# The expert layer's first matrix in 512-column passes, with the product banks handed out in pairs

## The chip, the core and the metric

The kernel runs on one core of one Trainium2 chip. The metric is the device time of one execution in microseconds (us), the median of several runs. The engines are called PE (matrix product), PEld (its weight loads), DVE (vector), ACT (scalar), POOL and SP; a line number such as L95 is a line of the kernel before.

## What is computed

Two transformer blocks on 256 tokens of width 1024, in float32. The last layer of the second block is a layer of 16384 experts, of which each token takes 16 for each of 8 heads:

```python
def peer_ffn(x, w_query, sub_keys, expert_u, expert_v):
    def block(xb):
        q = (xb @ w_query).reshape(PEER_TOKEN_BLOCK, PEER_HEADS, 2, PEER_HALF)
        sc = jnp.einsum('thpd,hpkd->thpk', q, sub_keys)
        s_top, i_top = lax.top_k(sc, PEER_TOPK)
        ...
        u = jnp.take(expert_u, eidx, axis=0)
        h = jax.nn.gelu(jnp.einsum('thkd,td->thk', u, xb))
        vv = jnp.take(expert_v, eidx, axis=0)
        return jnp.einsum('thk,thkd->td', g * h, vv)
```

The kernel does not gather experts. It multiplies the input with the whole of `expert_u` (the expert layer's first matrix, `peer_u`), applies gelu, multiplies each value with the gate of its token and expert (zero for those not chosen), and multiplies the result with the whole of `expert_v` (the second layer).

## The kernel before

**Products.** Every float32 operand is split into a high and a low part of type fp32r. A product is three matmuls into one accumulation (`mm3`, L108 to L112): high weight by high input (L110), high weight by low input (L111), low weight by high input (L112). The weights come in units of 128x1024 values: a DMA on SP's queue brings `raw`, ACT copies it to `whi` (L95), DVE forms the difference `wlo` (L96). There are 4 buffers for `raw`. Of `whi` and `wlo` there are 3 buffers in each of two pools up to the end of the second block's mixing part, and 3 in one pool in the expert layer: there the `whi` of a unit takes the buffer of the unit three places before it. `gemm_t` (L117) runs one unit: 8 slices k of 128 rows, 24 matmuls of 256 columns (the 256 tokens). `gemm_n` (L141) has the parts the other way round: the input is the stationary operand, and 512 columns of weights stream through.

**Banks.** A product goes to a bank of 512 float32 columns. `mm_bank` (L99) hands out four banks in turn, each a tile of its own; `ax_bank` four more for transposes, scores and sums. A bank is read out ("evicted") by DVE or ACT.

**Order.** A compiler pass (a list scheduler) writes the final order of each engine's instructions from the order in the program, the buffers and its own idea of durations; a tile's new user waits for the tile's earlier readers. On the chip each engine takes its instructions in that written order and holds at one whose semaphore count is not reached.

**The expert layer.** `first_layer(j)` (L994) runs unit j of `peer_u` (128 units of 128 experts) by `gemm_t`, two units into the two 256-column halves of one bank; after the odd one ACT applies gelu and writes `S` (L1009). Between the units run 16 query products (`query`, L955; read out by ACT as `qT`, L969), the score products on them, and the steps by which DVE chooses the experts (`pump`, `all_steps`). When the choice is done (`ready`), one-hot products (L942) form the gates of the first 128 tokens four at a time (`form`, `combine`): DVE and ACT build the operands, and DVE and ACT write the results into `S`. In this part the gelu of a pair is in two pieces (L1006, L1009), and DVE multiplies (L1007). The second layer (L1069) is 1536 matmuls of 512 columns into four `ax` banks.

**Other places named below.** L330 reads out a unit of the gate product of the first block (`gate`), L397 the gate and up products of its feed-forward part (`gu`), L291 the query, key and value products, L363 and its like the outputs of a projection (`xT`).

Of the kernel before, what the change touches and what calls it, by code (L numbers as in the profile page):

```python
# [7 lines left out]
F32 = mybir.dt.float32  # L8
F32R = mybir.dt.float32r
# [3 lines left out]
AF = mybir.ActivationFunctionType  # L13
OP = mybir.AluOpType
# [14 lines left out]
T = 256  # L29
TH = 128  # L30
# [10 lines left out]
NSMALL = _o  # L41


class Net:
    def __init__(self, tc, a, out, stack):
        self.tc, self.nc, self.a, self.out, self.stack = tc, tc.nc, a, out, stack
        nc = self.nc
        self.const = self.pool("const", 1)
        self.psum = self.pool("psum", 1, space=PSUM)
        self.tiny = self.pool("tiny", 2)  # L50
        self.small = self.const.tile([128, NSMALL], F32, name="small")
        nc.scalar.dma_start(out=self.small, in_=a["small"])
        self.ones = self.const.tile([128, 128], F32, name="ones")
        nc.vector.memset(self.ones, 1.0)
        warm = self.const.tile([128, 1], F32, name="warm")
        nc.scalar.activation(warm, self.ones[:, 0:1], AF.Exp)
        ps = self.ax_bank()
        for _ in range(WARM):
            nc.tensor.matmul(ps[:, :128], lhsT=self.ones, rhs=self.ones, start=True, stop=True)
# [21 lines left out]
    def unit_(self, src, n, pieces, engine, between):  # L81
# [17 lines left out]
                self.last_low = low.ins  # L99
        return hi, lo  # L100

    def mm_bank(self):
        return self.psum.tile([128, 512], F32, name="mm", bufs=4)

    def ax_bank(self, dt=F32):
        return self.psum.tile([128, 512], dt, name="ax", bufs=4)
# [1 line left out]
    def mm3(self, ps, left, right, first, last):  # L108
        mm = self.nc.tensor.matmul
        mm(ps, lhsT=left[0], rhs=right[0], start=first, stop=False)  # L110
        mm(ps, lhsT=left[0], rhs=right[1], start=False, stop=False)  # L111
        mm(ps, lhsT=left[1], rhs=right[0], start=False, stop=last)  # L112

    def acts(self, hl, k, ts=slice(0, T)):
        return hl[0][:, k, ts], hl[1][:, k, ts]
# [91 lines left out]
        return r  # L207

    def new_acts(self, pool, K=8, tag="act", bufs=2):
        return (pool.tile([128, K, T], F32R, tag=tag + "h", name=tag + "h", bufs=bufs),  # L210
                pool.tile([128, K, T], F32R, tag=tag + "l", name=tag + "l", bufs=bufs))

    def load_const(self, pool, name, shape):
        t = pool.tile(shape, F32, name=name)
# [20 lines left out]
    def block1(self, actp):  # L235
        nc, a, tc = self.nc, self.a, self.tc
        mult, add, sub = OP.mult, OP.add, OP.subtract
        with ExitStack():
# [6 lines left out]
            first = self.unit_(a["w_in_a"][0], 1024, 4, nc.gpsimd, load_x)  # L245
            h = self.new_acts(actp)
# [8 lines left out]
            both = self.const.tile([128, 192], F16, name="iota16")  # L255
# [4 lines left out]
            with ExitStack() as s1:  # L260
                p = self.pool("mix", 1, s1)
# [10 lines left out]
                for i, (dst, sc) in enumerate(dests):  # L272
                    ps = (self.ax_bank() if i in (3, 4) else self.mm_bank())[:, :T]
                    parts = first if i == 0 else None
                    if i == 1 or i == 2:
                        parts = self.unit(a["w_in_a"][i], 1024, pieces=2)
# [7 lines left out]
                    if i == 2:  # L284
                        r = self.norm_column(acc, "ra")
                    if i < 4:
                        continue
                    if i == 4:
                        R = self.rows(r, "ra")
# [6 lines left out]
                    if i == 5:  # L296
                        ps = self.ax_bank()
# [3 lines left out]
                        nc.scalar.activation(av.rearrange("p a b -> p (a b)"), ps[:, :T], AF.Copy)  # L301

                both = self.xbp.tile([128, 8, T], F32R, tag="xbh", name="att", bufs=1)
                att = both[:, 0:4], both[:, 4:8]
                probs = [self.att1_probs(p, tb, aq, ak, mask) for tb in range(2)]
                rv = p.tile([128, 2, D], F32, name="rv")
                room = p.tile([128, 8, 512], F32, tag="gate", name="room")
# [19 lines left out]
                for i in range(16):  # L327
                    ps = self.mm_bank()[:, :T]
# [8 lines left out]
                for m in range(8):  # L337
                    if m % 2 == 0:
                        hi, lo = self.unit(a["w_att_o"][m // 2], 1024)
                    ps = self.mm_bank()  # L340
                    for k in range(4):
                        s = slice((m % 2 * 4 + k) * 128, (m % 2 * 4 + k) * 128 + 128)
# [9 lines left out]
                h = self.new_acts(actp)  # L352
                acc = self.work.tile([128, T], F32, name="acc")
                for m in range(8):
# [3 lines left out]
                    if m < 2:  # L358
                        ps = two[m]
                    else:  # L360
                        ps = self.mm_bank()[:, :T]
# [4 lines left out]
            with ExitStack() as s1:  # L366
                p = self.pool("ffn", 1, s1)
# [8 lines left out]
                for f in range(KF):  # L376
                    ps = self.mm_bank()
                    if f == 0:
                        other = self.mm_bank()
                        self.gemm_t_late([(ps[:, :T], a["w_gate"][0]), (other[:, :T], a["w_up"][0])], h)  # L380
                        r = self.norm_column(acc, "rb")
# [3 lines left out]
                    if f == 2:  # L385
                        R = self.rows(r, "rb")
# [7 lines left out]
                    for f0, (g, u) in enumerate(early, f + 1 - len(early)):  # L394
                        gu = p2.tile([128, 2, T], F32, name="gu")
                        if f0:
                            nc.vector.tensor_tensor(out=gu, in0=g, in1=R[:, None, :].to_broadcast([128, 2, T]),  # L397
                                                    op=mult)
# [10 lines left out]
                h = self.new_acts(actp)  # L409
                acc = self.work.tile([128, T], F32, name="acc")  # L410
                acg = self.work.tile([128, T], F32, name="acg")
                for m in range(8):
                    ps = self.mm_bank()[:, :T]
# [303 lines left out]
    def peer(self, st, x3, h, acc):  # L717
        nc, a, tc = self.nc, self.a, self.tc
        mult, add, sub = OP.mult, OP.add, OP.subtract
        with tc.using_default_side("right"):  # L720
# [3 lines left out]
            late = ExitStack()  # L724
            p = self.pool("topk", 1, late)
            pick = p.tile([128, 3, 128], F32, name="pick")
        xb = self.new_acts(self.xbp, tag="xb", bufs=1)
        hand = self.pool("hand", 2, st)
        x3t = tc.dram_tile([2, 128, D], F32, name="x3t")
        stop = p.tile([128, 4, 2, 2, 16], F32, name="stop")  # L730
# [134 lines left out]
        ready = False  # L865

        def pump(budget):
            nonlocal credit
            credit = min(credit, 0) + budget
            while credit > 0:  # L870
                step = next(steps, 0)
                if step == 0:
                    return True
                if step is None:
                    return False
                step[1]()
                credit -= step[0]
            return False

        bank = None  # L880
# [67 lines left out]
                nc.scalar.activation(S[:, jd:, t0:t0 + 4], C[:, jd:], AF.Copy, scale=1.0 / GSCALE)  # L948
            done += 4

        pair, keys, r, R = None, None, None, None
        waiting = []
        firsts = []

# [37 lines left out]
                    nc.scalar.dma_start(out=x3t[c, :, k4 * 512:k4 * 512 + 512], in_=xt)  # L992

        def first_layer(j):  # L994
            nonlocal pair
            e = j % 2
            if e == 0:
                pair = self.mm_bank()
            self.gemm_t(pair[:, e * T:e * T + T], a["peer_u"][j], xb, 8)
            if e == 0:  # L1000
                return
            js = slice(j - 1, j + 1)
            p3 = pair.rearrange("p (e t) -> p e t", e=2)
            if done:
                gt = gtp.tile([128, 2, TH], F32, name="gt")
                nc.scalar.activation(gt[:, :, :done], p3[:, :, :done], AF.Gelu_apprx_tanh)  # L1006
                nc.vector.tensor_tensor(out=S[:, js, :done], in0=S[:, js, :done], in1=gt[:, :, :done], op=mult)  # L1007
            if done < T:
                nc.scalar.activation(S[:, js, done:], p3[:, :, done:], AF.Gelu_apprx_tanh)  # L1009

        for c in range(RAWQ):
            query(c)
            ready = pump(PQ)
# [18 lines left out]
        for j in range(128):  # L1032
            first_layer(j)
            if c < 16 and j % QE == QE - 1:
                query(c)
                c += 1
                pump(PQ)
            elif c == 16 and waiting:
                for one in waiting:
                    score(*one)  # L1040
                waiting.clear()
            if not ready:
                ready = pump(PU)
                if ready:
                    start = j
                    with tc.using_default_side("right"):
                        gtp = self.pool("gelu", 2, groups)
                        cp = self.pool("comb", 1, hots)
                    ga = cp.tile([128, TH], F32, name="ga")
                    nc.scalar.activation(ga, gs[:, 0], AF.Copy)  # L1050
            elif j % 2 and not fill:
                while done < TH and (done + len(formed) * 4) * (GP - start) < TH * (j - start):
                    combine(j + 1)
                if done == TH:
                    hots.close()
                    with tc.using_default_side("right"):
                        gp = self.pool("gates", 1, groups)
                    fill = [fetch(4 * i) for i in range(3)]
            if j == 121:
                apply(0, fill.pop(0))  # L1060
# [12 lines left out]
        for j in range(128):  # L1073
            w = self.unit(a["peer_v"][j], 1024)
            s = [qp.tile([128, T], F32R, tag=t, name=t, bufs=n) for t, n in (("keys", 2), ("q", 3))]
# [109 lines left out]
```

## Time and profile before

| | us |
|---|---|
| median of 3 runs (lowest, highest) | 1287.78 (1287.43, 1288.07) |
| the profiled execution's own time | 1289.19 |
| its span, first to last instruction | 1287.4 |
| PE busy | 1276.2 |
| DVE busy | 904.6 |
| ACT busy | 718.7 |
| choice of experts running beside the first matrix | about 523 to 731 of the span |
| first matrix after the choice | about 731 to 935 |
| second layer | about 935 to 1283 |

A row of the timeline gives the start in us from the span's start, the duration, the engine, the line, the operation with the tile written and those read, the sizes, and in brackets how long the engine had been idle and what ended that. The end of a matmul is modelled and matmuls overlap, so what a matmul costs is read from the distance between two starts. A row of the stretches gives for each engine its busy time and instructions, then the granted clock of PE (1.00 is 2.4 GHz), the busy share of the DMA engines and GB/s.

### The profile page before, as it was taken

The numbers are of one execution on the slowest core, as the hardware profiler recorded it, in microseconds if no ns is written. First come the engines' busy times: TensorE is split into PE (matmuls) and PEld (weight loads), VectorE is DVE, ScalarE is ACT, GpSimd is POOL, SyncE is SP. The second block draws the span as 40 slices with busy tenths as digits, with TensorE's granted clock in tenths as the row PEclk, the third lists the DMA queues.
The fourth block names the chain that finished last, engine by engine and source line by source line (L and its number), as shares of the span: only waits on it lengthen the run. The fifth ranks groups of instructions, "written<-read, shape, count | busy, mean of one in ns | idle before, by whom it ended". The sixth has DMA issues, their size and how long they took to land.

```text
span 1287.4 us, 23568 instructions
## 1 busy us (share of the span) xinstructions
PE 1276.2 (99%) x9125; PEld 1186.8 (92%) x9125; DVE 904.6 (70%) x1785; ACT 718.7 (56%) x1158; POOL 269.4 (21%) x173
## 2 busy tenths in 40 slices
PE   8999999999999999999999999999999999999998
PEld 7878999999999889999999999999988888888887
DVE  7767677766666886988895566776566666666665
ACT  5455545545455675655554676666555555555553
POOL 2000000000000000008778887773000000000000
PEclk9999999999999999999999999999999999999999
DMA  7745668965567544567777777776677777777764
GB/s 261 230 131 153 179 188 293 335 195 184 177 186 221 160 145 138 182 187 186 181 168 209 181 169 177 165 172 173 215 217 221 217 215 218 219 219 220 215 199 160
DMA packets 90928, 253.02 MB, mean 197 GB/s; under 512 B 26944, under 2 KB 28736, under 8 KB 90688
## 3 DMA queue, kind: packets, MB, share of 16 engines
q1 hardware_dynamic: 68816, 241.45, 61.0%
q0 software_dynamic: 20992, 8.46, 5.9%
q8 instruction: 71, 1.16, 0.4%
q10 hardware_dynamic: 1008, 1.61, 0.3%
q14 instruction: 41, 0.34, 0.1%
HBM read 240.93 MB, written 10.55 MB: 195 GB/s over the span
## 4 chain that ended last, share of the span: by engine, by line
PE 93%; DVE 5%; issue 1%; DMA 0%; ACT 0%; SPq 0%; ACTq 0%; DVEq 0%
PE ax L1069 27%; PE mm L110 21%; PE mm L112 20%; PE mm L111 20%; DVE wlo L96 2%; PE ax L942 1%; DVE itop L741 1%; PE ax L888 0%; DMA xT<-in_xT_dram 0%; DVE stop L739 0%; ACT whi L95 0%; DVE sc L744 0%; DVE pos L741 0%; PE ax L678 0%; PE ax L713 0%
## 5 line engine op out<-in xcount | busy, mean ns | idle before, releaser
L96 DVE TENSOR_TENSOR wlo<-raw,whi 128x1024 fp32r<-128x1024 f32 (+2 forms) x433 | 524.4, 1213 | 239.6 <-ACT whi L95 238.2
L95 ACT ACTIVATE whi<-raw 128x1024 fp32r<-128x1024 f32 (+3 forms) x439 | 457.9, 1045 | 313.2 <-PE mm L111 219.6
L110 PE MATMUL mm<-xbh,whi 128*128 128x256 f32 x1104 | 312.0, 283 | 0.0
L112 PE MATMUL mm<-xbh,wlo 128*128 128x256 f32 x1104 | 308.3, 279 | 0.3 <-DVE wlo L96 0.2
L111 PE MATMUL mm<-xbl,whi 128*128 128x256 f32 x1104 | 308.3, 279 | 0.2 <-DVE xbl L155 0.2
L832 POOL DMA_INDIRECT cmat<-best,pos x128 | 241.6, 1887 | 226.4 <-DVE itop L741 164.6
L110 PE MATMUL mm<-acth,whi 128*128 128x256 f32 x848 | 239.4, 282 | 3.0 <-DVE qkv L291 1.4
L111 PE MATMUL mm<-actl,whi 128*128 128x256 f32 x848 | 237.9, 281 | 1.5 <-DVE actl L253 1.5
L112 PE MATMUL mm<-acth,wlo 128*128 128x256 f32 x848 | 237.0, 280 | 0.0
L112 PEld LDWEIGHTS mm<-xbh,wlo 128*128 128x128 f32 x1104 | 207.4, 188 | 1.3 <-DVE wlo L96 0.9
L111 PEld LDWEIGHTS mm<-xbl,whi 128*128 128x128 f32 x1104 | 207.6, 188 | 0.4 <-DVE xbl L155 0.4
L110 PEld LDWEIGHTS mm<-xbh,whi 128*128 128x128 f32 x1104 | 207.6, 188 | 0.2 <-ACT xbh L154 0.2
L110 PEld LDWEIGHTS mm<-acth,whi 128*128 128x128 f32 x848 | 159.9, 189 | 4.3 <-DVE qkv L291 1.7
L111 PEld LDWEIGHTS mm<-actl,whi 128*128 128x128 f32 x848 | 160.1, 189 | 2.2 <-DVE actl L253 2.2
L112 PEld LDWEIGHTS mm<-acth,wlo 128*128 128x128 f32 x848 | 160.0, 189 | 0.2 <-DVE wlo L96 0.2
L1069 PE MATMUL ax<-whi,q 128*128 128x512 f32 x512 | 158.0, 389 | 0.0
L1069 PE MATMUL ax<-whi,keys 128*128 128x512 f32 x512 | 157.9, 389 | 0.0
L1069 PE MATMUL ax<-wlo,keys 128*128 128x512 f32 x512 | 157.9, 389 | 0.0
L154 ACT ACTIVATE keys<-S 128x256 fp32r<-128x256 f32 x128 | 53.5, 418 | 151.4 <-PE ax L1069 151.4
L1069 PEld LDWEIGHTS ax<-whi,q 128*128 128x128 f32 x512 | 96.1, 188 | 20.0
L1069 PEld LDWEIGHTS ax<-wlo,keys 128*128 128x128 f32 x512 | 96.1, 188 | 19.9
L1069 PEld LDWEIGHTS ax<-whi,keys 128*128 128x128 f32 x512 | 96.0, 188 | 20.0
(282 smaller groups left out, 1405.5 us busy)
## 6 DMA issues: line engine op xcount, KB each, us to landing
raw<-in_peer_u_dram SPq DMA_DIRECT2D x128, 512.0 KB
raw<-in_peer_v_dram SPq DMA_DIRECT2D x128, 512.0 KB
raw<-in_w_in_b_dram SPq DMA_DIRECT2D x32, 512.0 KB
raw<-in_w_in_a_dram SPq DMA_DIRECT2D x31, 512.0 KB
raw<-in_w_gate_dram SPq DMA_DIRECT2D x22, 512.0 KB
raw<-in_w_up_dram SPq DMA_DIRECT2D x22, 512.0 KB
raw<-in_w_out_dram SPq DMA_DIRECT2D x16, 512.0 KB
cmat<-zero SPq DMA_DIRECT2D x16, 512.0 KB
```

What stands on the lines that cost most here:

```text
L95: self.last_copy = nc.scalar.activation(hi[:, s], raw[:, s], AF.Copy).ins
L96: low = (engine or nc.vector).tensor_tensor(out=lo[:, s], in0=raw[:, s], in1=hi[:, s].bitcast(F32), op=OP.subtract)
L110: mm(ps, lhsT=left[0], rhs=right[0], start=first, stop=False)
L111: mm(ps, lhsT=left[0], rhs=right[1], start=False, stop=False)
L112: mm(ps, lhsT=left[1], rhs=right[0], start=False, stop=last)
L154: nc.scalar.activation(hi, src, AF.Copy)
L741: yield cost + 50, lambda: nc.vector.max_index(where[:, o:o + 8], top[:, o:o + 8], vals)
L832: i = nc.gpsimd.indirect_dma_start(self.cmat, bass.IndirectOffsetOnAxis(ap=ps[:, hd, 1, k:k + 1], axis=0), bs[:, hd, 1, k:k + 1], None, co ...
L942: nc.tensor.matmul(C[:, t * 128:t * 128 + 128], lhsT=A[:, t], rhs=G[i][:, t], start=i == 0, stop=i == 1)
L1069: nc.tensor.matmul(banks[tb][d], lhsT=s[left][:, ts], rhs=w[right][:, d * 512:d * 512 + 512], start=first, stop=end)
```

## The change

Three things change.

First, the high and the low part of an input stand side by side in one tile, for each k 256 columns of the high part and then 256 of the low (`new_acts`, `xb`, `att`).

Second, from the end of the choice of experts on, `first_layer` runs a unit by `gemm_w`: for each k one matmul of 512 columns (high weight, both parts) and one of 256 (low weight, high part). The two halves of the bank are added at the end: ACT copies the right halves of a pair of banks to `gt`, and DVE adds the left halves (`added`). Gelu then reads `gt`.

Third, the four product banks become two tiles of two banks each (`mm_pair`), each tile used in turn; `mm_bank` hands out the first bank of such a tile, then the second. This holds for the whole kernel.

```diff
+        self.half = None
...
+    def mm_pair(self):
+        self.half = None
+        return self.psum.tile([128, 2, 512], F32, name="mm", bufs=2)
+
     def mm_bank(self):
-        return self.psum.tile([128, 512], F32, name="mm", bufs=4)
+        if self.half is None:
+            pair = self.mm_pair()
+            self.half = pair[:, 1]
+            return pair[:, 0]
+        bank, self.half = self.half, None
+        return bank
...
+    def mm2(self, ps, weight, acts, k, first, last):
+
+        mm = self.nc.tensor.matmul
+        both = acts[2][:, k]
+        mm(ps, lhsT=weight[0], rhs=both, start=first, stop=False)
+        mm(ps[:, :T], lhsT=weight[1], rhs=both[:, 0], start=False, stop=last)
+
+    def gemm_w(self, ps, src, hl, K, k0=0, first=True, last=True):
+
+        hi, lo = self.unit(src, K * 128)
+        for k in range(K):
+            s = slice(k * 128, k * 128 + 128)
+            self.mm2(ps, (hi[:, s], lo[:, s]), hl, k0 + k, first and k == 0, last and k == K - 1)
+
+    def added(self, out, pair):
+
+        self.nc.scalar.activation(out, pair[:, :, T:], AF.Copy)
+        self.nc.vector.tensor_tensor(out=out, in0=pair[:, :, :T], in1=out, op=OP.add)
...
     def new_acts(self, pool, K=8, tag="act", bufs=2):
-        return (pool.tile([128, K, T], F32R, tag=tag + "h", name=tag + "h", bufs=bufs),
-                pool.tile([128, K, T], F32R, tag=tag + "l", name=tag + "l", bufs=bufs))
+        both = pool.tile([128, K, 2, T], F32R, tag=tag, name=tag, bufs=bufs)
+        return both[:, :, 0], both[:, :, 1], both
...
-            nonlocal pair
+            nonlocal pair, wide
             e = j % 2
             if e == 0:
-                pair = self.mm_bank()
-            self.gemm_t(pair[:, e * T:e * T + T], a["peer_u"][j], xb, 8)
+                wide = ready
+                pair = self.mm_pair() if wide else self.mm_bank()
+            if wide:
+                self.gemm_w(pair[:, e], a["peer_u"][j], xb, 8)
+            else:
+                self.gemm_t(pair[:, e * T:e * T + T], a["peer_u"][j], xb, 8)
             if e == 0:
                 return
             js = slice(j - 1, j + 1)
-            p3 = pair.rearrange("p (e t) -> p e t", e=2)
+            if wide:
+                p3 = gtp.tile([128, 2, T], F32, name="gt", bufs=1)
+                self.added(p3, pair)
+            else:
+                p3 = pair.rearrange("p (e t) -> p e t", e=2)
             if done:
-                gt = gtp.tile([128, 2, TH], F32, name="gt")
+                gt = p3 if wide else gtp.tile([128, 2, T], F32, name="gt", bufs=1)
```

In the changed program 68 units (60 to 127) run by `gemm_w`; that is 544 matmuls of 512 columns and 544 fewer matmuls in all.

The pairs of banks move PE's instructions in the whole kernel. The rows below are the written order; names carry the number of the buffer's use, and the brackets name the engine whose count an instruction waits for.

The first place is PE in the last third of the choice of experts. `mm_7761` is a tile of two banks; `whi_7806` and `wlo_7807` are the last unit of its first bank, `whi_7845` the first unit of its second bank, and `whi_7919` a unit of the next tile, the third unit after `whi_7806`. In the changed program:

```order
L131 MATMUL mm_7761<-xb_5837,whi_7806 128x256
L132 MATMUL mm_7761<-xb_5837,wlo_7807 128x256
L130 MATMUL mm_7917<-xb_5836,whi_7919 128x256 [waits Activation_49]
L131 MATMUL mm_7917<-xb_5836,whi_7919 128x256
L130 MATMUL mm_7761<-xb_5836,whi_7845 128x256 [waits Activation_49]
L131 MATMUL mm_7761<-xb_5836,whi_7845 128x256
L132 MATMUL mm_7761<-xb_5836,wlo_7846 128x256 [waits DVE_49]
```

In the program before, PE goes there from one bank to the next one:

```order
L111 MATMUL mm_8070<-xbl_5896,whi_8113 128x256
L112 MATMUL mm_8070<-xbh_5895,wlo_8114 128x256
L110 MATMUL mm_8150<-xbh_5895,whi_8152 128x256 [waits Activation_49]
L111 MATMUL mm_8150<-xbl_5896,whi_8152 128x256
L112 MATMUL mm_8150<-xbh_5895,wlo_8153 128x256 [waits DVE_49]
```

Two matmuls of a later unit now stand ahead of the second bank's first matmul, and that first matmul waits for ACT: the count that it waits for is that of the ACTIVATE that reads the first bank.

The second place is ACT there, in the changed program. `S_6172<-mm_7761` reads the first bank (the one that PE waits for); `whi_7919` is the copy that the two early matmuls wait for, and its own wait for PE is for the last matmul on `whi_7806`, whose buffer it takes:

```order
L937 ACTIVATE sc_7794<-ax_7749 128x512 [waits PE_49]
L106 ACTIVATE whi_7919<-raw_7918 128x1024 [waits DMAHW1_49,DVE_49,PE_49]
L1058 ACTIVATE S_6172<-mm_7761 128x512 [waits PE_49]
L106 ACTIVATE whi_7956<-raw_7955 128x1024 [waits DMAHW2_49,DVE_49,PE_49]
L106 ACTIVATE whi_7995<-raw_7994 128x1024 [waits DMAHW3_49,DVE_49,PE_49]
```

In the program before, ACT's order at such a place is the same (a copy, then the read-out):

```order
L95 ACTIVATE whi_8113<-raw_8112 128x1024 [waits DMAHW4_49,DVE_49,PE_49]
L95 ACTIVATE whi_8152<-raw_8151 128x1024 [waits DMAHW5_49,DVE_49,PE_49]
L1009 ACTIVATE S_6234<-mm_7993 128x512 [waits PE_49]
L95 ACTIVATE whi_8189<-raw_8188 128x1024 [waits DMAHW6_49,DVE_49,PE_49]
L95 ACTIVATE whi_8226<-raw_8225 128x1024 [waits DMAHW7_49,DVE_49,PE_49]
```

ACT's order has not moved there; what has moved is what PE holds at.

The third place is PE in the gate product of the first block. `mm_1341` is a tile of two banks, `whi_1343` the unit of its first, `whi_1374` that of its second, `mm_1404` the next tile. In the changed program:

```order
L132 MATMUL mm_1341<-act_122,wlo_1344 128x256
L130 MATMUL mm_1404<-act_122,whi_1406 128x256 [waits DVE_49,Activation_49]
L131 MATMUL mm_1404<-act_122,whi_1406 128x256
L132 MATMUL mm_1404<-act_122,wlo_1407 128x256
L130 MATMUL mm_1404<-act_122,whi_1406 128x256
L131 MATMUL mm_1404<-act_122,whi_1406 128x256
L130 MATMUL mm_1341<-act_122,whi_1374 128x256 [waits DVE_49]
```

Before, a unit's last matmul is followed by the next unit's first:

```order
L110 MATMUL mm_1322<-acth_122,whi_1324 128x256
L111 MATMUL mm_1322<-actl_123,whi_1324 128x256
L112 MATMUL mm_1322<-acth_122,wlo_1325 128x256
L110 MATMUL mm_1355<-acth_122,whi_1357 128x256 [waits DVE_49]
L111 MATMUL mm_1355<-actl_123,whi_1357 128x256
```

Here five matmuls of the next tile stand between the banks of one tile, and the second bank's first matmul waits for the DVE instruction that reads the first bank.

## Rows read from the trace of the kernel before

**Rows 1.** The page: busy time of the engines, and PE's granted clock in 40 slices.

```profile
PE 1276.2 (99%) x9125; PEld 1186.8 (92%) x9125; DVE 904.6 (70%) x1785; ACT 718.7 (56%) x1158; POOL 269.4 (21%) x173
...
PEclk9999999999999999999999999999999999999999
```

**Rows 2.** The page: the chain that ended last, by engine.

```profile
PE 93%; DVE 5%; issue 1%; DMA 0%; ACT 0%; SPq 0%; ACTq 0%; DVEq 0%
```

**Rows 3.** The waits of PE: waited for, us in total, times, longest.

```profile
PE mm L111 <- DVE actl L253: 1.5, 3, 0.7
...
PE mm L110 <- ACT whi L95: 0.5, 1, 0.5
PE mm L112 <- DVE wlo L96: 0.2, 1, 0.2
```

**Rows 4.** Stretches: first block's gates, choice of experts, rest of the first matrix.

```profile
130.00:230.00 100.00, 100.00 (x860) 100.00 (x859) 70.41 (x114) 51.93 (x68) 0.96 (x1) 1.00 0.72 226
...
523.00:680.00 157.00, 156.49 (x1323) 155.15 (x1322) 143.19 (x579) 85.76 (x113) 81.15 (x44) 1.00 0.69 179
...
731.00:935.00 204.00, 204.00 (x1866) 202.78 (x1865) 137.91 (x228) 133.20 (x292) 120.59 (x72) 1.00 0.73 179
```

**Rows 5.** Timeline of PE, first matrix: matmuls of 256 columns, first and 37th.

```profile
907.42 0.28 PE L110 MATMUL mm<-xbh,whi 128*128 128x256 f32 x1
...
911.63 0.28 PE L110 MATMUL mm<-xbh,whi 128*128 128x256 f32 x1
```

**Rows 6.** Timeline of PE, a `gemm_n`: matmuls of 512 columns, first and 28th.

```profile
64.33 0.40 PE L112 MATMUL mm<-whi,actl 128*128 128x512 f32 x1
...
70.63 0.40 PE L112 MATMUL mm<-whi,actl 128*128 128x512 f32 x1
```

**Rows 7.** Timeline of PE, second layer: matmuls of 512 columns, first and 49th.

```profile
1000.38 0.61 PE L1069 MATMUL ax<-whi,keys 128*128 128x512 f32 x2
...
1011.26 0.61 PE L1069 MATMUL ax<-whi,keys 128*128 128x512 f32 x2
```

**Rows 8.** Timeline of PE at the end of a unit in the choice of experts.

```profile
688.36 0.28 PE L111 MATMUL mm<-xbl,whi 128*128 128x256 f32 x1
688.47 0.28 PE L112 MATMUL mm<-xbh,wlo 128*128 128x256 f32 x1
688.59 0.28 PE L110 MATMUL mm<-xbh,whi 128*128 128x256 f32 x1
```

**Rows 9.** Timeline of ACT at the same place, and at a query and a table load.

```profile
639.90 1.28 ACT L1009 ACT_TABLE_LOAD   x1
...
641.81 1.05 ACT L95 ACTIVATE whi<-raw 128x1024 fp32r<-128x1024 f32 x1
642.76 0.37 ACT L969 ACTIVATE qT<-mm 128x256 f32<-128x256 f32 x1
...
688.67 1.06 ACT L95 ACTIVATE whi<-raw 128x1024 fp32r<-128x1024 f32 x1 [1.74 <-PE mm L111]
689.64 0.58 ACT L1009 ACTIVATE S<-mm 128x512 f32<-128x512 f32 x1
```

**Rows 10.** Timelines of PE and DVE where PE holds for a read-out and starts again.

```profile
28.46 0.28 PE L112 MATMUL mm<-acth,wlo 128*128 128x256 f32 x1
30.19 0.39 PE L110 MATMUL mm<-acth,whi 128*128 128x256 f32 x1 [1.45 <-DVE qkv L291]
30.41 0.28 PE L111 MATMUL mm<-actl,whi 128*128 128x256 f32 x1
...
29.71 1.08 DVE L291 SCALAR_TENSOR_TENSOR qkv<-mm,ra 128x256 f32<-128x256 f32 x3
```

**Rows 11.** Timelines of PE and DVE at the end of a gate unit, and DVE's `gu`.

```profile
139.80 0.28 PE L112 MATMUL mm<-acth,wlo 128*128 128x256 f32 x1
...
140.12 0.43 DVE L330 TENSOR_TENSOR gate<-mm,ra 128x256 f32<-128x256 f32 x1 [0.55 <-PE mm L112]
141.15 1.23 DVE L96 TENSOR_TENSOR wlo<-raw,whi 128x1024 fp32r<-128x1024 f32 x1 [0.60 <-ACT whi L95]
...
284.27 0.69 DVE L397 TENSOR_TENSOR gu<-mm,rb 128x512 f32<-128x512 f32 x1 [0.46 <-PE mm L112]
```

**Rows 12.** One line's instructions: ACT's read-out of 512 columns with a scale.

```profile
L557 ACT ACTIVATE qraw<-mm,rd x4: 684/687/692, 429.0 to 433.2; 128x512 f32<-128x512 f32 x4
```

More of the change, by code (lines that the diff above doesn't have):

```diff
@@ L41, with __init__, __getitem__ @@
 NSMALL = _o
+class Halves:
+    def __init__(self, parts):
+        self.parts = parts
+    def __getitem__(self, at):
+        return self.parts[at[1] // 4][(at[0], at[1] % 4, *at[2:])]
 class Net:
@@ L303, in block1 @@
                 both = self.xbp.tile([128, 8, T], F32R, tag="xbh", name="att", bufs=1)
-                att = both[:, 0:4], both[:, 4:8]
+                both = both.rearrange("p (k e) t -> p k e t", e=2)
+                att = both[:, :, 0], both[:, :, 1], both
                 probs = [self.att1_probs(p, tb, aq, ak, mask) for tb in range(2)]
@@ L726, in peer @@
             pick = p.tile([128, 3, 128], F32, name="pick")
-        xb = self.new_acts(self.xbp, tag="xb", bufs=1)
+        parts = [self.xbp.tile([128, 4, 2, T], F32R, tag=t, name="xb", bufs=1) for t in ("xbl", "xbh")]
+        xb = [Halves([x[:, :, i] for x in parts]) for i in range(2)] + [Halves(parts)]
         hand = self.pool("hand", 2, st)
@@ L949, in combine @@
             done += 4
-        pair, keys, r, R = None, None, None, None
+        pair, keys, r, R, wide = None, None, None, None, False
         waiting = []
```

## The prediction

> **What bounds the kernel now.** I read the page first. PE is busy 1276.2 of 1287.4 us with the granted clock at nine tenths or more in every slice [rows 1], 1.00 (2.4 GHz) in the stretches [rows 4], and 93% of the chain that ended last is PE [rows 2]. The waits of PE come next: the longest group is 1.5 us in all [rows 3]. So the time is PE's own matmuls one behind the other. Two things can move it: what a matmul costs, and every hold of PE that is new. The stretches say how much room the other engines have: DVE is busy 143.2 of 157 us (91%) while the experts are chosen, and after it 137.9 of 204, ACT 133.2 of 204 [rows 4].
>
> **The wide pass.** 68 units now take 16 matmuls each, where they took 24: 544 passes of 512 columns for 1088 of 256. A pass of 256 costs (911.63 - 907.42) / 36 = 0.117 us [rows 5]. In `gemm_n` one of 512 costs (70.63 - 64.33) / 27 = 0.2333, just twice that [rows 6]; in the second layer (1011.26 - 1000.38) / 48 = 0.2267 [rows 7]. So the pass brings 544 x (0.2333 - 0.2339) = nothing by the first price, and 544 x 0.007 = 3.9 us by the second; if the remaining 544 low passes also fell to half the second layer's price (0.1133) it would be 5.9. I take nothing: in `gemm_n`, as here, every matmul changes its weights and all go to one bank. The bounds are 0 and -5.9; as a loss nothing speaks for it, since the same columns pass.
>
> A page bears on this. The Trainium skill, "TensorE: Matmul & The Clock Gate", section "Back-to-back issue gap", gives each matmul N / 2.4 ns and a fixed part of about 2.5 ns; by that 544 fewer matmuls would bring an estimate of 1.4 us. The rows of `gemm_n` show no such part, those of the second layer a larger one; the sum goes by the rows.
>
> **The added copies and adds.** 34 ACT copies and 34 DVE adds of 512 values a partition. By the nearest rows a read-out of 512 columns takes 0.69 us on DVE [rows 11] and 0.687 on ACT [rows 12]: 34 x 0.69 = 23.5 us for each. In 731 to 935 that makes DVE (137.9 + 23.5) / 204 = 79% and ACT 77%: they lie beside PE. PE would see them only where it wants the tile back, and it comes back to it after a whole other tile, 32 matmuls of 5.6 us, against a copy and an add of 1.4 us. Without that cover they would cost up to 34 x 1.4 = 47 us; it is there, so 0. The parts side by side I cost at nothing: the same instructions write them, at another address, and PE is what they would have to delay; one that ran longer would do so beside PE as the copies do.
>
> **The banks in pairs.** This is the part that the words of the change pass over. Before, a bank was a tile, and four in turn gave PE three whole banks of work before it needed one back. Now two banks are one tile, and the written order makes the first matmul on the second bank wait for the instruction that reads the first. That instruction can start only after the first bank's last matmul. So PE holds from there to the end of the read-out, less the matmuls of the next tile that stand ahead as cover. In the changed order I count 64 places where PE waits so; 41 of them have less cover than the wait takes (18 behind ACT, 23 behind DVE), in the others the matmuls ahead reach. The wide part has none, since there both banks are read at the end. The price of a place depends on what else stands ahead of the read-out on its engine.
>
> *Read-outs by ACT, in the choice of experts.* The order shows a `whi` copy ahead of the read-out, and that copy takes the buffer of the unit PE has just finished. From the last high matmul to the copy's start it is 688.67 - 688.36 = 0.31 [rows 8, 9]; from there to the read-out's start 689.64 - 688.67 = 0.97; the read-out of `S` takes 0.58 [rows 9]. From a read-out's end to PE's start it is 30.19 - (28.46 ... 29.71 + 0.42, the last of the three) = 0.06 to 0.07, and the restart costs 30.41 - 30.19 = 0.22 where 0.12 is usual, so 0.10 more [rows 10]. PE would have gone on 2 x 0.117 after that high matmul. A place costs 0.31 + 0.97 + 0.58 + 0.07 + 0.10 - 0.23 = 1.80 less its cover. For `qT` the read-out is 0.37 and the copy to read-out 642.76 - 641.81 = 0.95 [rows 9]: 1.57 less its cover.
>
> Cover in the written order, per place, at 0.117 a matmul:
> - ten `S` places: three with 2 matmuls (1.57 each), one with 3 (1.45), one with 4 (1.33), four with ten (0.63), one with 13 (0.28): 10.3 us;
> - six `qT` places: two with 6 matmuls (0.87 each), one with 5 (0.98), three with 11 (0.28): 3.6 us;
> - two `S` places where a table load of 1.28 [rows 9] stands in between, so 3.08 less 21 and 25 matmuls: 0.8 us.
>
> Together 14.7 us: 8.8 in the last seven places, 655 to 731, and 5.9 before.
>
> *Read-outs by DVE, in the two blocks.* A gate unit's last matmul starts at 139.80, its read-out at 140.12 for 0.43 [rows 11]: 0.32 + 0.43 + 0.07 + 0.10 - 0.12 = 0.80, less five matmuls, 0.59: 0.21 for each of six places, 1.3 us. `gu` reads 512 columns in 0.69 [rows 11]: 1.06 less eight matmuls (0.94) is 0.12 in nine places, 1.1 us. Eight single ones of the same kind (three of the down projection at 0.21, one of `xT` at 0.33, four more at 0.2) make 1.6. Together 4.0 us. Below, a place costs nothing (its cover reaches); above, the read-out is late by a `wlo` ahead of it in DVE's queue, rival A.
>
> What queues behind a holding PE is only later matmuls; ACT's next copy and DVE's `wlo` wait for buffers that PE frees, so they come later too, and the DMA queue with them: nothing else gains from it. Where PE already had short gaps in the choice (156.49 of 157, and the 0.5 and 0.2 us of [rows 3]) a hold can swallow them, at most 2.3 us; I take 1.0 off.
>
> **Sum.** 14.7 + 4.0 - 1.0 + 0 = +17.7 us on the profiled execution's 1289.19: 1306.9. That execution is 1.4 us above the median of 1287.78; so the forecast is 1305.5.
>
> A rule speaks for the other side. The Trainium skill, "PSUM — Partial Sum Buffer", on bank collisions, asks for a guard where PE writes and another engine reads the same bank. By it the chip itself would allow PE to write the second bank while the first is read. No run here shows whether the chip would; in this program the wait is written down, by tile, and the written order is what PE follows.
>
> **Rivals.** The measurement can tell about 0.2%, 2.6 us, from no change.
>
> *A, more than that: DVE's read-outs stand behind a `wlo`.* At the fifteen gate and `gu` places the read-out shares DVE's queue with differences of 1.23 us [rows 11]. DVE is 70% busy there [rows 4]. If the difference comes first in time, most places cost about 1 us more: 15 x (0.7 to 1.2) = 11 to 18, so 1316 to 1324. Against it: before, DVE was idle for 0.55 us when the gate's bank was ready [rows 11]. Chance 0.10.
>
> *B, less: in the first part of the choice DVE sets the pace.* At 91% busy [rows 4], PE's holds before 680 only replace waits for DVE, and the eleven early places (5.9) cost nothing: 1305.5 - 5.9 = 1299.6. Against it: PE itself is busy 156.49 of the same 157. Chance 0.13.
>
> *C, not slower: the holds are as short as the bare read-out, and the wide pass pays for them.* Place: the same eighteen holds. If the copies found their buffers early, a place would cost the read-out alone less its cover: for `S` 0.31 + 0.58 + 0.07 + 0.10 - 0.23 = 0.83, so three of 0.6, one of 0.48, one of 0.36, the rest nothing, 2.6 us; `qT` by the same sum is nothing, and DVE's places are 0 to 4.0: 2.6 to 6.6 in all. Against that stands the pass at the second layer's price, 3.9 to 5.9. It decides from the point where the holds sum to less than the pass brings: 1287.8 + 2.6 - 5.9 = 1284.5, up to 1287.8 + 6.6 - 3.9 = 1290.5. Against it: the copy's own wait for the unit just finished is in the written order, and the nearest price of the pass is the one that brings nothing. Chance 0.12: 0.05 faster, 0.07 the same.
>
> That the wide pass isn't taken is none: the order shows the 544.
>
> **How the numbers follow.** The forecast has 0.65. Its own range: down by the pass at 3.9 and the full 2.3 us of swallowed gaps, with covers that hide most of DVE's 4.0, 1305.5 - 3.9 - 1.3 - 4.0 = 1296; up by the read-outs that start later by 0.3 in a third of the 64 places, 6.4: 1312. B lies inside it. To leave out no more than 2 in 10 the range must hold the near edges of A and of C's neighbourhood: 1293 to 1316. Slower by over 0.2%: 0.65 + 0.10 + 0.13 = 0.88; the same 0.07, faster 0.05.
>
> **What would show it.** Right: PE's waits name ACT's read-outs of `S` and `qT`, each above a microsecond, and DVE's `gate` and `gu` with tenths; 523 to 731 grows by about 15 us, 731 to 935 stays at 204 with 512-column starts 0.233 apart; DVE and ACT are busy 23 us more in all. Wrong: the starts are 0.227 apart and that part is 4 us shorter; or PE's waits stay as they were, which would fell the whole sum; or DVE appears with a microsecond at each gate (A).

## The result and the profile after

The changed kernel takes 1323.1 us (median of 4 runs, 1322.14 to 1324.66), the kernel before 1287.92 in the same series: 1.0273 times, 95% interval 1.0259 to 1.0287. The prediction said slower, by 17.7 us; it is 35.2. The time lies above the range of 1293 to 1316.

The page of the changed kernel, busy time of the engines, answers to [rows 1]; behind it the chain that ended last, which answers to [rows 2]:

```profile
PE 1290.3 (98%) x8581; PEld 1167.9 (88%) x8581; DVE 927.1 (70%) x1819; ACT 740.3 (56%) x1192; POOL 270.8 (20%) x173
...
PEclk8999999999999899999999999999999999999999
...
PE 87%; DVE 9%; ACT 1%; DMA 1%; issue 1%; POOL 0%; ACTq 0%; DVEq 0%; POOLq 0%
```

544 matmuls fewer, and the span is 33.8 us longer, 1321.2 for 1287.4. DVE and ACT are busy 22.5 and 21.6 us more (the copies and adds), and PE's share of the chain falls: 87% where it was 93%. The waits of PE show where it holds now (waited for, us in total, times, longest); before, none was above 1.5 [rows 3]:

```profile
PE mm L130 <- ACT whi L106: 5.8, 8, 1.0
PE ax L238 <- ACT dg L237: 3.4, 1, 3.4
PE mm L132 <- DVE wlo L107: 3.3, 4, 1.7
PE mm L130 <- ACT qraw L597: 3.1, 1, 3.1
...
PE ax L888 <- DVE pick L851: 2.1, 1, 2.1
...
PE mm L130 <- DVE u L644: 1.4, 2, 0.7
```

Where along the program the time was lost is read best by a landmark that both programs have. ACT makes 439 copies `whi` in either program. Counted from 0, the start of the k-th in one trace less its start in the other, each from the start of its span, is the lag that has gathered by then (0.3 us at copy 0). By that count, against the kernel before:

| up to copy | place | changed kernel | gained there |
|---|---|---|---|
| 144 | first block | +4.4 | +4.4 |
| 150 | second block, norm of q and k | +13.6 | +9.3 |
| 174 | rest of the second block | +18.2 | +4.6 |
| 240 | choice of experts | +36.5 | +18.3 |
| 318 | rest of the first matrix, wide | +33.8 | -2.7 |
| 438 | second layer | +33.8 | 0 |

**A hold for `S`.** PE in the choice, the timeline at one of the places with two matmuls of cover, and ACT at the same place:

```profile
672.25 0.27 PE L132 MATMUL mm<-xb,wlo 128*128 128x256 f32 x1
673.55 0.38 PE L130 MATMUL mm<-xb,whi 128*128 128x256 f32 x1 [1.03 <-ACT whi L106]
673.78 0.28 PE L131 MATMUL mm<-xb,whi 128*128 128x256 f32 x1
674.04 0.39 PE L130 MATMUL mm<-xb,whi 128*128 128x256 f32 x1
674.26 0.28 PE L131 MATMUL mm<-xb,whi 128*128 128x256 f32 x1
```

```profile
672.45 1.06 ACT L106 ACTIVATE whi<-raw 128x1024 fp32r<-128x1024 f32 x1 [1.59 <-PE mm L131]
673.41 0.58 ACT L1058 ACTIVATE S<-mm 128x512 f32<-128x512 f32 x1
```

From 672.25 four matmuls on is 674.26, 2.01 us; at 0.117 each it would be 0.47. The hold is 1.54, and the sum said 1.57. The view of waits books 1.03 of it to the copy. It is the read-out behind the copy that ends it (673.41 + 0.58 = 673.99, PE starts at 674.04), but by little: the two matmuls that stand ahead as cover need that copy themselves, and after them PE would have gone on at 673.78 + 0.117 = 673.90.

**The norm.** PE, ACT and DVE at 424 to 437, timelines:

```profile
424.44 0.58 PE L227 MATMUL ax<-ones,acg 128*128 128x1 f32 x4
428.45 0.78 PE L238 MATMUL ax<-dg,ones 128*128 128x128 f32 x4 [3.43 <-ACT dg L237]
432.31 0.80 PE L130 MATMUL mm<-whi,act 128*128 128x512 f32 x1 [3.08 <-ACT qraw L597]
...
433.75 0.63 PE L130 MATMUL mm<-whi,act 128*128 128x512 f32 x1
...
435.04 0.63 PE L130 MATMUL mm<-whi,act 128*128 128x512 f32 x1
...
436.31 0.40 PE L130 MATMUL mm<-whi,act 128*128 128x512 f32 x1
```

```profile
428.00 0.69 ACT L237 ACTIVATE dg<-ident,rcc 128x128 f32<-128x128 f32 x2 [2.62 <-DVE rcc L212]
...
431.57 1.27 ACT L597 ACTIVATE qraw<-mm,rd 128x512 f32<-128x512 f32 x2 [1.92 <-DVE rd L582]
```

PE had run out of work from 424.4 on. Its next product (`k`, the L130 at 432.31) starts in the second half of a tile whose first half holds a bank of `q`, and the read-out of that bank, `qraw`, is multiplied by `rd`, the end of a chain of small DVE steps that is ready only at 431.5. Before, two other banks were free, and `k` ran beside the chain. After the two pauses the matmuls of 512 columns (three to an L130) stand (435.04 - 433.75) / 3 = 0.43 us apart up to 436.31, and 0.23 from there on. The granted clock there is 0.52, half of 2.4 GHz; in the kernel before it was 1.00 from 400 to 523. The changed kernel, then the kernel before:

```profile
430.00:436.50 6.50, 4.19 (x10) 3.36 (x11) 4.24 (x19) 2.88 (x6) 0.00 (x0) 0.52 0.00 1
```

```profile
400.00:523.00 123.00, 123.00 (x904) 112.37 (x903) 95.20 (x218) 80.32 (x152) 0.52 (x1) 1.00 0.53 167
```

**The wide pass.** PE's timeline right after the choice, the first and the 64th of 63 rounds of one 512-column and one 256-column matmul that nothing interrupts; then the stretches (columns as in [rows 4]) that answer to 523 to 731 and 731 to 935:

```profile
765.90 0.40 PE L138 MATMUL mm<-xb,whi 128*128 128x512 f32 x1
...
787.74 0.39 PE L138 MATMUL mm<-xb,whi 128*128 128x512 f32 x1
```

```profile
541.00:767.00 226.00, 214.41 (x1774) 208.94 (x1773) 173.25 (x626) 118.08 (x168) 134.38 (x68) 0.99 0.66 169
767.00:968.60 201.60, 201.60 (x1306) 177.11 (x1306) 155.62 (x246) 144.63 (x305) 111.33 (x65) 1.00 0.71 183
```

A round is (787.74 - 765.90) / 63 = 0.3467 us, against 3 x 0.117 = 0.3508 by [rows 5]: 0.0041 x 544 = 2.2 us gained, and PE is busy in the whole second stretch.

### The profile page after: what moved, and what is told of

Same layout as the page of the kernel before. It is cut to its first block, busy times and chain, and to the rows that moved or that the text cites. A ratio compares the mean times of both kernels' runs of the same rounds, so it can differ in the third digit from the quotient of the medians.

```text
span 1321.2 us, 22589 instructions
## 1 busy us (share of the span) xinstructions
PE 1290.3 (98%) x8581; PEld 1167.9 (88%) x8581; DVE 927.1 (70%) x1819; ACT 740.3 (56%) x1192; POOL 270.8 (20%) x173
## 4 chain that ended last, share of the span: by engine, by line
PE 87%; DVE 9%; ACT 1%; DMA 1%; issue 1%; POOL 0%; ACTq 0%; DVEq 0%; POOLq 0%
PE ax L1118 26%; PE mm L130 15%; PE mm L132 14%; PE mm L131 14%; PE mm L138 9%; PE mm L139 5%; DVE wlo L107 3%; PE ax L983 1%; DVE itop L782 1%; ACT whi L106 1%; DMA raw<-in_w_in_a_dram 1%; DVE stop L780 1%; DVE oh L848 0%; DVE sc L785 0%; DMA small<-in_small_dram 0%
## 5 line engine op out<-in xcount | busy, mean ns | idle before, releaser
L130 PE MATMUL mm<-act,whi 128*128 128x256 f32 x848 | 241.3, 286 | 4.4 <-DVE qkv L330 1.7
L131 PE MATMUL mm<-act,whi 128*128 128x256 f32 x848 | 238.0, 281 | 2.5 <-DVE act L292 2.3
L132 PE MATMUL mm<-act,wlo 128*128 128x256 f32 x848 | 234.6, 280 | 0.0
L138 PE MATMUL mm<-xb,whi 128*128 128x512 f32 x544 | 192.0, 394 | 0.0
L130 PEld LDWEIGHTS mm<-act,whi 128*128 128x128 f32 x848 | 160.3, 190 | 9.5 <-DVE qkv L330 1.9
L130 PE MATMUL mm<-xb,whi 128*128 128x256 f32 x560 | 159.1, 285 | 6.0 <-ACT whi L106 5.8
L131 PEld LDWEIGHTS mm<-act,whi 128*128 128x128 f32 x848 | 160.6, 189 | 3.6 <-DVE act L292 3.1
L132 PEld LDWEIGHTS mm<-act,wlo 128*128 128x128 f32 x848 | 159.4, 189 | 0.0
L132 PE MATMUL mm<-xb,wlo 128*128 128x256 f32 x560 | 155.4, 282 | 3.4 <-DVE wlo L107 3.3
L131 PE MATMUL mm<-xb,whi 128*128 128x256 f32 x560 | 157.0, 281 | 0.0
L139 PE MATMUL mm<-xb,wlo 128*128 128x256 f32 x544 | 153.1, 281 | 0.0
L138 PEld LDWEIGHTS mm<-xb,whi 128*128 128x128 f32 x544 | 102.1, 188 | 20.6
L130 PEld LDWEIGHTS mm<-xb,whi 128*128 128x128 f32 x560 | 105.9, 189 | 9.3 <-ACT whi L106 8.0
```

Of the source, the lines that this page charges most:

```text
L138: mm(ps, lhsT=weight[0], rhs=both, start=first, stop=False)
L139: mm(ps[:, :T], lhsT=weight[1], rhs=both[:, 0], start=False, stop=last)
```

## The experiments

Theory: the loss is the tie between the two halves of a tile, and the wide pass is a small gain. All ratios are to the kernel before in the same series.

**1. The tie alone.** The kernel before with the new `mm_pair` and `mm_bank`, and nothing else:

```diff
     def mm_bank(self):
-        return self.psum.tile([128, 512], F32, name="mm", bufs=4)
+        if self.half is None:
+            pair = self.mm_pair()
+            self.half = pair[:, 1]
+            return pair[:, 0]
+        bank, self.half = self.half, None
+        return bank
```

> The kernel before with nothing but the product banks handed out as halves of two tiles. Theory (the loss is the tie of the two banks, the wide pass brings about 3 us): slower than the changed kernel, not only by the wide pass's 2.7 us: in the rest of the first matrix the written order has 18 more places where a second bank waits for the read-out of the first, most with 18 short matmuls ahead (1.15 us), so 15 x 0.65 + 3 x 1.57 = 14 us: about 1323 + 3 + 14 = 1340. Rival 1 (those places have enough cover): 1326. Rival 2 (the loss comes from the wide pass, its copies and adds, or from the input parts side by side): 1288.

Measured: 1339.85 us, 1.0401 (1.0383 to 1.0418). Its lag is that of the changed kernel up to the end of the choice (+4.3, +13.8, +18.4, +36.7 at the landmarks of the table), and then it loses 13.6 us more where the changed kernel gains 2.7. So the wide pass, the copies, the adds and the new layout have no part in the loss. The price of a place, 1.80 less its cover, held for 18 places that were not in the prediction: 14 expected, 13.6 found.

**2. The wide pass alone.** The changed kernel with four tiles of one bank:

```diff
-                pair = self.mm_pair() if wide else self.mm_bank()
+                pair = (self.mm_bank(), self.mm_bank()) if wide else self.mm_bank()
...
+        for e in range(2):
+            self.nc.scalar.activation(out[:, e], pair[e][:, T:], AF.Copy)
+            self.nc.vector.tensor_tensor(out=out[:, e], in0=pair[e][:, :T], in1=out[:, e], op=OP.add)
```

> The changed kernel with four banks that are tiles of their own; a wide pair takes two of them, copied and added bank by bank (68 copies and 68 adds of 256 columns instead of 34 of 512). Theory (the tie of the banks is the whole loss): all 36 us come back and the wide pass's 2.7 stay gained: about 1285. Rival (part of the loss is in the new layout of the input parts or in the copies and adds): 1288 to 1300.

Measured: 1285.82 us, 0.9986 (0.9976 to 0.9995). From copy 20 to the end of the choice the lag stays within 0.4 us of zero, and it is -2.1 at the end of the first matrix: 2.0 us gained in the wide part, none lost elsewhere. The parts side by side cost nothing, as forecast.

**3. Another parity at the norm.** The changed kernel with one line more, ahead of the product `q`:

```diff
+            self.half = None
             raw = {"q_g": self.gemm_n(a["w_in2_b"][0], h)}
```

> The changed kernel, but the first product of the second block's mixing part starts on a fresh tile, so that its two banks are the two halves of one tile (in the changed kernel it has the second half of one and the first half of the next, and the next product's first matmul then waits for a read-out that needs the norm). Theory (the norm's chain is laid bare there): the 9.3 us between 423 and 451 go, some of the 4.6 behind it too, later places change little (about as many, at other units): 1310 to 1315. Rival (PE would stand there for the norm in any case, because the scheduler moved the norm's own matmuls ahead): 1320 to 1323.

Measured: 1309.61 us, 1.0167 (1.015 to 1.0184). The lag is +4.7 at copy 144 and +4.7 at copy 150: the 9.3 us are gone, with no work taken away. The read-out at that place still waits for `rd`; PE doesn't wait for the read-out:

```profile
433.69 1.27 ACT L598 ACTIVATE qraw<-mm,rd 128x512 f32<-128x512 f32 x2 [1.54 <-DVE rd L583]
```

The rest of the second block costs 2.4 instead of 4.6 and the choice 16.2 instead of 18.3; that other units now share a tile is the likely reason, not a shown one. By these two it came out 0.4 us below the expected range.

**4. Two banks, no halves.** The changed kernel, but the narrow parts use only the first bank of a tile:

```diff
     def mm_bank(self):
-        if self.half is None:
-            pair = self.mm_pair()
-            self.half = pair[:, 1]
-            return pair[:, 0]
-        bank, self.half = self.half, None
-        return bank
+        return self.mm_pair()[:, 0]
```

> The changed kernel, but outside the wide part only the first bank of each tile is used: two banks in all, no halves. Theory (what costs is the tie between the halves, not how many banks there are): a bank then has a whole unit or two ahead of its reuse (24 to 48 matmuls, 2.8 to 5.6 us), so the gates' 4 us and the choice's 18 us go, and the place at the norm stays, since its second product wants back the banks of the first: 1297 to 1303. Rival (it is the number of free banks): 1323 or more.

Measured: 1313.22 us, 1.0201 (1.0182 to 1.0219), 10 us above what I expected; the parts tell why. In the choice it loses 0.2 us (25.5 at copy 174, 25.7 at 240) where the changed kernel loses 18.3, though it has half as many banks: there it is the tie, not the number. At the norms it is the number. The norm of `q` and `k` costs 9.6, as foreseen, and a norm of the first block (`dg`, at 235 us) some 9 that I had not foreseen. Some 6 more go at the start of the first block, 4.0 of them in a wait for `wlo` whose reason I have not followed. The changed kernel loses neither there. Its two longest waits of PE, the first at the two norms:

```profile
PE ax L232 <- ACT dg L231: 8.3, 2, 4.9
PE ax L126 <- DVE wlo L107: 4.0, 1, 4.0
```

**5 and 6. Is DVE late in the choice?** The places in the choice summed to 14.7 less 1.0, and 18.3 were lost. To see whether the rest is DVE, its `wlo` were left out, once with the halves tied and once with four tiles:

```diff
-        lo = wpar.tile([128, 1024], F32R, name="wlo")
+        lo = hi if self.nolow else wpar.tile([128, 1024], F32R, name="wlo")
...
             else:
+                self.nolow = j > 0
                 self.gemm_t(pair[:, e * T:e * T + T], a["peer_u"][j], xb, 8)
+                self.nolow = False
```

> The changed kernel (halves tied), but for the units 1 to 59 of the first matrix DVE's difference wlo is left out, and the low pass takes the high part again, so PE's matmuls and ACT's copies stay as many. It takes some 70 us of work off DVE while the experts are chosen. Theory (of the 18.3 us that the choice lost, about 12 are the holds for ACT's read-outs, and the rest is DVE: its wlo stand in its queue behind the holds, so the steps of the choice come late and PE then waits for wlo, 3.3 us, and for pick, 2.1 us and 1.5 us at the lower clock): 1323 - 7 = 1316. Rival (all of the 18.3 are the holds themselves): 1322 to 1323.

> The same omission in the kernel with four banks as tiles of their own (the second run): what leaving wlo out is worth where no halves are tied. Theory (PE sets the time there and DVE is never late): 1285 to 1286, as with wlo. Rival (DVE at 91% already costs PE some time in the choice): 1282 to 1284.

Measured: 1316.85 us tied (1.0223, 1.0207 to 1.0238), as the theory said, and 1284.21 with four tiles (0.9972, 0.9961 to 0.9983), below what its theory said and within its rival. From copy 174 to 240 the tied one loses 11.4 us where the changed kernel lost 18.3, and the one with four tiles gains 2.3 where the second run gained 0.2. So of the 18.3, the difference of the two, 6.9 - 2.1 = 4.8 us, is DVE's lateness that comes only with the holds; the 2.1 are what DVE's `wlo` cost without any tie, in short gaps of PE of which the view of waits names 0.5 behind DVE. Of PE's waits for `wlo` and `pick` only one of 0.6 us is left in that stretch of the tied one; the waits for ACT remain:

```profile
PE mm L133 <- ACT whi L107: 6.5, 8, 1.2
PE mm L135 <- DVE wlo L110: 0.6, 1, 0.6
```

Tied and with `wlo` (the changed kernel), PE and DVE where the choice of the experts ends look so:

```profile
699.26 0.39 PE L130 MATMUL mm<-xb,whi 128*128 128x256 f32 x1 [1.03 <-ACT whi L106]
699.49 0.28 PE L131 MATMUL mm<-xb,whi 128*128 128x256 f32 x1
701.84 0.44 PE L888 MATMUL ax<-ident,pick 128*128 128x128 f32 x2 [2.07 <-DVE pick L851]
```

```profile
698.95 1.22 DVE L107 TENSOR_TENSOR wlo<-raw,whi 128x1024 fp32r<-128x1024 f32 x1
...
701.60 0.18 DVE L851 CAST pick<-oh 128x32 f32<-128x32 f16 x1
```

A hold of 1.0 us for a copy is followed at once by one of 2.1 for the last `pick`, 701.60 + 0.18 against a start at 701.84. That DVE fell behind because its `wlo` stand in its queue until the held PE frees a buffer for the copy is the likely way; the runs show that `wlo` and holds together make it late, not each step of it.

**7. Why 0.2333 in `gemm_n`?** The second run's kernel with `gemm_n`'s two banks in turn:

```diff
+            for k in range(2):
+                s = slice(k * 512, k * 512 + 512)
+                for n, (x, y) in enumerate(((0, hi), (0, lo), (1, hi))):
+                    for tb in range(2):
+                        self.nc.tensor.matmul(banks[tb], lhsT=hl[x][:, 2 * q + k, tb * 128:tb * 128 + 128],
```

> The second run's kernel with gemm_n's 384 passes of 512 columns in another order: the two banks in turn, with the same streamed weights twice in a row, as in the second layer. It asks why a pass of 512 costs 0.2333 us there and 0.227 in the second layer. Theory (the order of banks and streamed operands): passes 0.227 apart, 2.5 us off: 1283.3. Rival (something else, such as what the other engines do meanwhile): 1285.8, 0.233 apart.

Measured: 1286.07 us, 0.9989 (0.998 to 0.9998), the same as the second run, and the passes stand 0.233 us apart on average, as before. The theory falls. The wide pass has a median distance of 0.228 with one bank and new weights each time, the two marks by which I had put it beside `gemm_n`. What sets the 6 ns stays open.

**8. More of the wide pass.** The second run's kernel with all 128 units wide:

```diff
-                wide = ready
+                wide = True
...
-                p3 = gtp.tile([128, 2, T], F32, name="gt", bufs=1)
+                p3 = gtp.tile([128, 2, T], F32, name="gt", bufs=1) if ready else S[:, js]
```

> The second run's kernel with all 128 units of the first matrix in the wide pass, those beside the choice of experts too (the sum and gelu are made in place in S there). 480 more passes of 512 at 0.006 less: -2.8 us if the 60 more copies and adds are hidden: 1283. Rival: DVE, busy 169 of 208 us there, gets 60 x 0.43 = 26 us more, 94%, and PE waits for its wlo and for the choice's end: 1288 to 1300. I expect the rival, about 1290.

Measured: 1282.7 us, 0.996 (0.9946 to 0.9974): faster than both kernels, and my guess of 1290 was wrong. The choice gains 2.7 us (lag -1.2 at copy 174, -3.9 at 240) and the rest of the first matrix 2.6. Its stretches:

```profile
523.00:731.00 208.00, 207.89 (x1294) 186.78 (x1293) 189.43 (x677) 131.44 (x217) 119.93 (x68) 1.00 0.74 186
731.00:930.00 199.00, 199.00 (x1305) 174.64 (x1304) 159.75 (x290) 150.55 (x352) 111.21 (x66) 1.00 0.72 182
```

DVE is busy 189 of 208 us, and the view of PE's waits names none in that stretch. So 91% is no limit by itself where PE isn't stopped; in the changed kernel, with 173.25 of 226 us in the same part (77%), DVE was late.

## Why the prediction was wrong

The direction, the mechanism and its places were right: "PE holds from there to the end of the read-out". The first and second run show it, the tie alone giving more than the whole loss and the change without it a small gain. Rival C did not happen, since the holds last through the copy as the sum said, nor A: the first block's places behind DVE cost about what was said, no microsecond each. Nor did B, by which the early part of the choice would have cost nothing: it cost 5.8 us (copy 174 to 216). That 5.9 were summed for its eleven places is luck, though. PE's waits in that part of the changed kernel (541 to 672) are for DVE in the main, where the sum had read-outs by ACT:

```profile
PE mm L132 <- DVE wlo L107: 3.3, 4, 1.7
PE mm L130 <- ACT whi L106: 0.6, 2, 0.4
```

The sign that was named, waits for the read-outs of `S` and `qT`, each above a microsecond, did not come either: the view names the copies (5.8 us in eight).

What failed is the size, term by term:

- **The norm, forecast 0.2, measured 9.3.** The step is "That instruction can start only after the first bank's last matmul. So PE holds from there to the end of the read-out", by which every place got a price; this one had at most a share of "four more at 0.2". I priced the read-out of `q` as if it could start when its bank was full. It needs `rd`, a DVE chain that ends 7 us after PE's last statistics matmul (424.44 to 431.54), and PE's whole next product had covered it before. The loss is 3.4 + 3.1 us of pause and some 2 us at the lower clock. The third run takes exactly this away. It is the largest error, over half of the 16 us that were missing (33.8 less 17.7 by the profiles).
- **The rest of the second block, forecast 0.2 to 0.4, measured 4.6.** The waits name `u` (1.4 in two), `act` (0.9 in two) and `xT` (0.2), where before they named 0.2 in all; no run takes them apart further. The other parity halves it (2.4 in the third run).
- **The choice, forecast 14.7 - 1.0, measured 18.3.** The holds for ACT were priced well where DVE is out of the way: 1.54 against 1.57 at the one shown, and 11.4 + 2.3 = 13.7 us between the fifth and the sixth run, against 14.7. "Nothing else gains from it", I wrote of what queues behind a holding PE; something else loses. DVE came late by 4.8 us (fifth and sixth run) and PE then held for `wlo` and `pick`. No run shows the 1.0 that I took off for swallowed gaps: PE's waits for DVE there grew.
- **The first block, forecast some 3.5, measured 4.4** (0.3 of it before the first copy). Near enough.
- **The wide pass, forecast 0, measured -2.0 to -2.7** (second run, changed kernel). It lies between the two prices. Choosing the `gemm_n` price by likeness was a guess that the trace did not bear out; as a term it is small.
- **The copies and adds, forecast hidden.** Right: PE is busy in all of 767 to 968.6, and the eighth run hides 60 more beside a busier DVE.

Three slips in the working matter little. The eight single places add up to 1.8, not 1.6. The bound of 2.3 us for swallowed gaps does not follow from the rows beside it (0.5 us of idle in 157). And the read-out that ends 0.06 us before PE's start in [rows 10] is the first of the three, not the last.

The Trainium skill's rule in "TensorE: Matmul & The Clock Gate", section "Back-to-back issue gap", gave an estimate of 1.4 us for the 544 matmuls saved; the section states it for a matmul by itself, which the prediction left out. The second run measures 2.0: the sign was right and the size nearer than the zero I took.

## What to carry to other kernels

A tile of two banks is one thing to the waits of this program: PE doesn't fill one half while the other is read. Before tying buffers, ask of each read-out not how long it takes but what it waits for, and how much of the old order's work covered that. Ask of the matmuls that stand ahead as cover what they wait for, too. A read-out that needs a late scalar turned a hold priced at 0.2 us into a loss of nine. Where a wide pass needs two banks, two single tiles give it the same gain without the tie.

## What was not expected

- A pause of PE costs more than its length: after 6.5 us of waiting the passes of 512 columns stood 0.43 apart instead of 0.23 for 4 us more, near half the speed, at a granted clock of 0.52 (1.2 of 2.4 GHz). The Trainium skill, "TensorE: Matmul & The Clock Gate", section "Back-to-back issue gap", gives N / 1.2 ns for a matmul by itself at the lower level, an estimate of 426.7 ns for 512 columns; the trace agrees with 0.43 us.
- The same banks in pairs can cost 9.3 us at one place or nothing, by which half a product starts in (third run).
- DVE at 91% busy left PE without a wait that the view names (eighth run), and at 77% it held PE (the changed kernel): its share of busy time says little where its queue is held.
- A pass of 512 columns takes 0.233 us in `gemm_n`, 0.228 in the wide pass and 0.227 in the second layer; the order of banks in `gemm_n` doesn't change its 0.233 (seventh run).
